# Six buffers for the conditioning rows, loads five tasks ahead, and VectorE's paced operations held in program order

## The chip, the cores and the metric

The kernel runs on one core of one Trainium2 chip. The metric is the device time of one execution in microseconds. In this text the engines are called as the profile calls them: PE is TensorE (PEld its weight loads), DVE is VectorE, ACT is ScalarE, POOL is GpSimd, and SP is SyncE, which here only issues DMAs. L152 is line 152 of the kernel.

## The reference

A two-layer diffusion backbone works on 256 latent tokens of width 2048, with 256 context tokens beside them. Everything is float32. Layer 0 mixes tokens by neighbourhood attention (16 heads), layer 1 by a gated MLP whose spatial weights mix positions in chunks of 128. Each mixer is followed by a SwiGLU FFN of inner width 5632. Every sub-layer is modulated by a condition vector c:

```python
sh1, sc1, g1, sh2, sc2, g2 = split(silu(c) @ ada_w[i] + ada_b[i], 6)
h = layer_norm(ALPHA * h + g1 * mixer(h * (1 + sc1) + sh1), ...)
h = layer_norm(ALPHA * h + g2 * swiglu(h * (1 + sc2) + sh2), ...)
```

The modulation itself is a product of one vector with a matrix of 2048 x 12288 per layer. That matrix is 100 MB per layer, and reading it is a large part of the kernel's 606 MB of traffic from HBM.

## The kernel before, in words

**The main work.** PE multiplies in three passes: each operand is split into a high part (a cast by ACT, L93) and a low part (a subtraction by DVE, L94), and `mm3` (L87 to L90) multiplies high by high, high by low and low by high. Weights stream in as pieces of 128 x 1024 numbers, 512 KB each. SP loads a piece into one of four raw buffers (L110), ACT and DVE split it, and PE uses it in twelve or more matmuls. `piece()` hands out one piece and calls `prefetch`, so that in the code the split of a piece stands four pieces ahead of its use (two during attention, since `pos["bufs"]` is 3 there and 5 later). Activations are split by `act_split` into `gh` and `gl`, with four buffers each.

**The stages.** First come the early products with the first modulation (0 to about 160 us), then attention head by head (to about 600), the output projection, the first FFN (`pg`, `pu`, then `pod`, to about 1411), the gated MLP (`gv`, `gu`, `pogo`, to about 1713) and the second FFN. At the end of each `project_out` the residual, the layer norm and the next modulation run on DVE and ACT, and PE needs their result.

**The paced tasks.** The rest of the modulation is done in small steps beside the main work. There are two kinds of task. A `dot_task` loads 512 KB of the matrix (tile `ad`, L77) and multiplies it with the broadcast condition row, summing over the row (L152). A `gate_task` loads 512 KB (tile `ag`, L77) and adds it, scaled by one column, to a gate tile (L176); after 32 of them a `sum_task` adds up the gate's partitions on POOL (L191). There are 192 tasks of the first kind and 128 of the second. All their loads go through ACT's DMA queue into tiles with the tag `ada`, of which there are four. `junk` (L335) and the tiles `e` in `project_out` share that tag, at other times.

`add_tasks` fills a list at four places in the code: the start of attention, the first FFN, the gated MLP and the second FFN. `tick()` is called after the products of a piece. It adds credit at a rate set by `pace` and runs tasks while there is credit; when `side` holds other work (row-wise affine work, transposes) it runs one item of that and counts 0.3 of a tick. `need(...)` runs all tasks that are left of the named vectors at once. `fetch_ahead` issues the loads of the first `FETCH` tasks of the list.

**What sets the order.** The code is only a list of instructions. When the program is built, a planner gives each engine a fixed order. It goes by priority (the order in the code, or ahead of it inside `tc.high_priority`) and by the times at which it assumes that inputs are there. An instruction that is ready may pass earlier ones that are not. `pin` (`keep_in_program_order`) forbids one thing: a pinned instruction is not placed ahead of the instruction that precedes it in the code on its own engine. Other instructions may still pass a pinned one. In the kernel before, the loads of the tasks are pinned on ACT (L77), most weight loads of the first stage are pinned on SP, and the DVE operations of the tasks are not pinned. [...]

[...]

Of the kernel before, what the change touches and what calls it, by code (L numbers as in the profile page):

```python
# [15 lines left out]
ALU = mybir.AluOpType  # L16
# [21 lines left out]
SH1, SC1, G1, SH2, SC2, G2 = range(6)  # L38
HK0 = 3
RAW = 4  # L40
ADA = 4
FETCH = 3
BUSY = 0.3
DVE0 = 3
W0 = HK0 * P + 512
# [6 lines left out]
def hybrid_kernel(ctx: ExitStack, tc: tile.TileContext, i, out):  # L52
    nc = tc.nc
    V, S, T = nc.vector, nc.scalar, nc.tensor
# [3 lines left out]
    c_col = outer.tile([P, KT, 2], F32, tag="ccol", name="c_col")  # L58
# [16 lines left out]
    def load(src, name):  # L75
        r = outer.tile([P, 1024], F32, tag="ada", name=name, bufs=ADA)
        tc.keep_in_program_order(nc.scalar.dma_start(r, src))  # L77
        return r
# [5 lines left out]
    def pin(ins):  # L84
        return tc.keep_in_program_order(ins)
# [54 lines left out]
    loaded = {}  # L140

    def dot_task(layer, t, nt, half):
        key = (layer, t, nt, half)

        def fetch():
            src = i["ada_t"][dot_index(layer, t, nt)]
            loaded[key] = load(src[:, half * 1024 : (half + 1) * 1024], f"ad{layer}{t}{nt}{half}")

        def run():
            r = loaded.pop(key)  # L150
            o = (cols2 if half else cols)[:, layer, t, :]
            V.scalar_tensor_tensor(  # L152
                r, r, 1.0, c_bc[:, half * 1024 : (half + 1) * 1024], ALU.mult, ALU.mult,
                accum_out=o[:, nt : nt + 1],
            )
            if nt == KT - 1 and half:
                o = cols[:, layer, t, :]
                V.tensor_tensor(o, o, cols2[:, layer, t, :], ALU.add)
                V.tensor_tensor(o, o, badj[:, layer, t, :], ALU.add)
        return [(layer, t), 0.5, run, fetch]  # L160

    def gate_task(layer, t, kt, half):
        key = (layer, t, kt, half)
        sl = slice(half * 1024, (half + 1) * 1024)

        def fetch():
            if kt == 0 and half == 0:
                g = outer.tile([P, D], F32, tag="gate", name=f"gate{layer}{t}")
                gate[(layer, t)] = g
                nc.gpsimd.memset(g, 0.0)  # L170
                nc.gpsimd.dma_start(g[0:1, :], i["ada_b_row"][layer, t : t + 1, :])
            loaded[key] = load(i["ada_g"][gate_index(layer, t, kt)][:, sl], f"ag{layer}{t}{kt}{half}")

        def run():
            g = gate[(layer, t)][:, sl]
            V.scalar_tensor_tensor(g, loaded.pop(key), c_col[:, kt, 0:1], g, ALU.mult, ALU.add)  # L176
        return [(layer, t), 0.5, run, fetch]

    def act_split(src, name, at=None):
# [17 lines left out]
    def fetch_ahead():  # L197
        for t in tasks[:FETCH]:
            if t[3]:
                t[3]()  # L200
                t[3] = None
# [75 lines left out]
    with tc.tile_pool(name="attnX", bufs=1) as px, ExitStack() as late:  # L277
# [21 lines left out]
        with tc.tile_pool(name="st", bufs=1) as st:  # L299
# [33 lines left out]
            def dot_dve(kt, t):  # L333
                r = held.pop((kt, t))
                junk = outer.tile([P, D], BF16, tag="ada", name=f"junk{kt}", bufs=ADA)  # L335
                for n, (o, bc) in enumerate(((junk, cc_bc), (r, c_bc))):
# [358 lines left out]
    def project_out(kts, src, key, name, finish, extra, last=False):  # L695
        st = stats_tile(name)
        hold = LAST if last else HOLD
        for nh in range(2):
# [10 lines left out]
            def fetch(kt, n):  # L709
                xs = []  # L710
                for k in range(n):
                    at = None
                    if k >= START:
                        if k % 2 == 0:
                            e = outer.tile([P, 4, NT], F32R, tag="ada", name=f"e{name}{k}", bufs=ADA)
                        at = e[:, 2 * (k % 2), :], e[:, 2 * (k % 2) + 1, :]
# [223 lines left out]
def dot_index(layer, t, nt):  # L940
    return DOT[(layer, t, nt)]


def gate_index(layer, t, kt):
    return (layer * 2 + (t == G2)) * KT + kt
# [94 lines left out]
```

## Time and profile before

| | |
|---|---|
| time, median of 3 runs | 2462.59 us (2460.63 to 2463.62) |
| the profiled execution: its time, its span | 2464.19 us, 2462.4 us |
| PE busy | 2388.5 us (97%) |
| DVE busy | 1753.7 us (71%) |
| ACT busy | 1120.5 us (46%) |
| mean granted clock of PE | 0.991 |
| read from HBM | 606.46 MB, 247 GB/s over the span |

The span is the time from the first to the last instruction in the profile. The profiler writes down when each instruction started and ended, which semaphore released it and how long its engine stood idle before it. Ends of matmuls are modelled, so two matmuls in a row overlap in the rows. A row of a group ends with the idle time of the engine just before the group's instructions and with what ended it; a row of the timeline has the same in brackets. A row of a stretch of time lists the busy microseconds of each engine in it, the granted clock of PE as a share of full speed, the share of time in which the DMA engines moved data, and the rate. Idle time of an engine costs nothing as long as the engine that sets the time has work.

### The profile page before, as it was taken

To read this page: it belongs to the slowest core of one execution; us is meant where nothing else is said; L and a number is where in the kernel's file an instruction comes from. 1 tells how busy PE (TensorE), PEld (TensorE's weight loads), DVE (VectorE), ACT (ScalarE), POOL (GpSimd) and SP (SyncE) were. 2 spreads that over 40 slices of the span, in tenths; PEclk is the share of its full clock that TensorE was granted. 3 is DMA by queue.
4 is the path that set the end of the run, shared out by engine and by line. 5 is a ranking of instruction groups with operands and counts; after the bars stand their busy time and mean duration, and the time that the engine had idled before them with its cause. 6 is when DMAs were issued, how large, how long until landed. Compare 5 with 4: busy or idle time off the path is not lost. (4 is left out here: it accounts for less than half of the span.)

```text
span 2462.4 us, 31266 instructions
## 1 busy us (share of the span) xinstructions
PE 2388.5 (97%) x11574; PEld 1979.4 (80%) x11574; DVE 1753.7 (71%) x2158; ACT 1120.5 (46%) x1534; POOL 110.3 (4%) x54
## 2 busy tenths in 40 slices
PE   7999999999999999999999999899999999999998
PEld 5788888888788888887888778777888888888886
DVE  4878877777887777666778778778755555566666
ACT  3344434335554444443455554445544444445453
POOL 0000200000010010000000010020100000020000
PEclk9999999999999999999999999999999999999999
DMA  9978787877578888887888767766567676766563
GB/s 358 346 248 266 254 288 260 273 253 246 188 241 284 293 280 299 284 290 275 280 290 283 247 208 263 241 210 196 199 229 229 226 227 225 230 198 190 178 211 131
DMA packets 167682, 610.63 MB, mean 248 GB/s; under 512 B 19076, under 2 KB 21572, under 8 KB 163172
## 3 DMA queue, kind: packets, MB, share of 16 engines
q1 hardware_dynamic: 120888, 440.64, 53.9%
q10 hardware_dynamic: 46512, 167.96, 19.9%
q8 instruction: 90, 1.47, 0.2%
q14 instruction: 64, 0.52, 0.1%
q0 software_dynamic: 128, 0.03, 0.0%
HBM read 606.46 MB, written 2.10 MB: 247 GB/s over the span
## 5 line engine op out<-in xcount | busy, mean ns | idle before, releaser
L93 ACT CAST hwf<-rwf 128x1024 fp32r<-128x1024 f32 x320 | 336.9, 1053 | 491.2 <-PE pu L90 206.0
L94 DVE TENSOR_TENSOR lwf<-rwf,hwf 128x1024 fp32r<-128x1024 f32 x320 | 404.3, 1277 | 173.8 <-ACT hwf L93 172.8
L152 DVE SCALAR_TENSOR_TENSOR ad<-ad,c_bc 128x1024 f32<-128x1024 f32 x192 | 234.0, 1222 | 168.9 <-DMA ad<-in_ada_t 168.3
L88 PE MATMUL pod<-hwd,ghd 128*128 128x512 f32 x684 | 267.3, 391 | 3.5 <-DVE sg L815 3.5
L90 PE MATMUL pod<-hwd,gld 128*128 128x512 f32 x684 | 266.5, 390 | 0.7 <-DVE gld L94 0.7
L89 PE MATMUL pod<-lwd,ghd 128*128 128x512 f32 x684 | 266.8, 390 | 0.0
L176 DVE SCALAR_TENSOR_TENSOR gate<-ag,c_col,gate 128x1024 f32<-128x1024 f32 x128 | 164.4, 1288 | 121.1 <-DMA ag<-in_ada_g 120.8
L94 DVE TENSOR_TENSOR lwd<-rwd,hwd 128x1024 fp32r<-128x1024 f32 x172 | 211.7, 1232 | 51.3 <-ACT hwd L93 51.0
L93 ACT CAST hwd<-rwd 128x1024 fp32r<-128x1024 f32 x172 | 180.3, 1049 | 33.3 <-PE pu L90 11.5
L88 PEld LDWEIGHTS pod<-hwd,ghd 128*128 128x128 f32 x684 | 128.7, 188 | 30.5 <-DVE sg L815 4.0
L90 PEld LDWEIGHTS pod<-hwd,gld 128*128 128x128 f32 x684 | 128.7, 188 | 28.1 <-DVE gld L94 1.2
L89 PEld LDWEIGHTS pod<-lwd,ghd 128*128 128x128 f32 x684 | 128.8, 188 | 26.6
L88 PE MATMUL pg<-hwf,f1h 128*128 128x512 f32 x320 | 126.4, 395 | 0.0
L88 PE MATMUL pg<-hwf,f0h 128*128 128x512 f32 x320 | 126.4, 395 | 0.0
L90 PE MATMUL pg<-hwf,f1l 128*128 128x512 f32 x320 | 124.7, 390 | 0.0
L90 PE MATMUL pg<-hwf,f0l 128*128 128x512 f32 x320 | 124.7, 390 | 0.0
L88 PE MATMUL pu<-hwf,f0h 128*128 128x512 f32 x320 | 124.5, 389 | 0.0
L89 PE MATMUL pu<-lwf,f0h 128*128 128x512 f32 x320 | 124.5, 389 | 0.0
L90 PE MATMUL pu<-hwf,f0l 128*128 128x512 f32 x320 | 124.5, 389 | 0.0
L88 PE MATMUL pu<-hwf,f1h 128*128 128x512 f32 x320 | 124.5, 389 | 0.0
L89 PE MATMUL pu<-lwf,f1h 128*128 128x512 f32 x320 | 124.5, 389 | 0.0
L90 PE MATMUL pu<-hwf,f1l 128*128 128x512 f32 x320 | 124.5, 389 | 0.0
(338 smaller groups left out, 5345.1 us busy)
## 6 DMA issues: line engine op xcount, KB each, us to landing
rwf<-in_w_in_t SPq DMA_DIRECT2D x320, 512.0 KB
ad<-in_ada_t ACTq DMA_DIRECT2D x192, 512.0 KB
rwd<-in_w_out SPq DMA_DIRECT2D x176, 512.0 KB
ag<-in_ada_g ACTq DMA_DIRECT2D x128, 512.0 KB
rwg<-in_w_gin SPq DMA_DIRECT2D x64, 512.0 KB
ap<-in_ada_p SPq DMA_DIRECT2D x19, 1024.0 KB
rwq<-in_w_q SPq DMA_DIRECT2D x32, 512.0 KB
rwo<-in_w_o SPq DMA_DIRECT2D x32, 512.0 KB
```

Of the source, the lines that this page charges most:

```text
L88: keep(T.matmul(ps, sh, mh, start=first, stop=False))
L89: keep(T.matmul(ps, sh, ml, start=False, stop=False))
L90: keep(T.matmul(ps, sl, mh, start=False, stop=last))
L93: S.copy(hi, src)
L94: V.tensor_tensor(lo, src, hi.bitcast(F32), ALU.subtract)
L152: V.scalar_tensor_tensor(r, r, 1.0, c_bc[:, half * 1024 : (half + 1) * 1024], ALU.mult, ALU.mult, accum_out=o[:, nt : nt + 1],)
L176: V.scalar_tensor_tensor(g, loaded.pop(key), c_col[:, kt, 0:1], g, ALU.mult, ALU.add)
```

## The change

The tag `ada` gets six buffers instead of four, which takes 8 KB more of each partition, and `FETCH` is 5 instead of 3. [...] The DVE operations of both kinds of task are wrapped in `pin`.

```diff
-ADA = 4
-FETCH = 3
+ADA = 6
+FETCH = 5
+SCRATCH = 4096
...
-            V.scalar_tensor_tensor(
+            pin(V.scalar_tensor_tensor(
                 r, r, 1.0, c_bc[:, half * 1024 : (half + 1) * 1024], ALU.mult, ALU.mult,
                 accum_out=o[:, nt : nt + 1],
-            )
+            ))
...
-            V.scalar_tensor_tensor(g, loaded.pop(key), c_col[:, kt, 0:1], g, ALU.mult, ALU.add)
+            pin(V.scalar_tensor_tensor(g, loaded.pop(key), c_col[:, kt, 0:1], g, ALU.mult, ALU.add))
...
-    nc = bacc.Bacc("TRN2", target_bir_lowering=False, num_devices=1)
+    nc = bacc.Bacc("TRN2", target_bir_lowering=False, num_devices=1, dynamic_dma_scratch_size=SCRATCH)
```

## The prediction

> **What bounds the kernel now.** I read the shares of the engines first, then the groups of the paced operations, then the stages, then the places where PE stands still. The page:
>
> ```profile
> PE 2388.5 (97%) x11574; PEld 1979.4 (80%) x11574; DVE 1753.7 (71%) x2158; ACT 1120.5 (46%) x1534; POOL 110.3 (4%) x54
> ...
> L152 DVE SCALAR_TENSOR_TENSOR ad<-ad,c_bc 128x1024 f32<-128x1024 f32 x192 | 234.0, 1222 | 168.9 <-DMA ad<-in_ada_t 168.3
> ...
> L176 DVE SCALAR_TENSOR_TENSOR gate<-ag,c_col,gate 128x1024 f32<-128x1024 f32 x128 | 164.4, 1288 | 121.1 <-DMA ag<-in_ada_g 120.8
> ```
>
> PE sets the time. The 320 paced operations of VectorE (DVE) that the change touches make DVE wait 168.3 + 120.8 = 289.1 us for their loads, but a wait of DVE costs only where PE then runs dry. By stage (columns: stretch, length, busy us and instructions of PE, PEld, DVE, ACT, POOL, clock, DMA share, GB/s):
>
> ```profile
> 164.00:700.00 536.00, 514.77 (x2746) 441.41 (x2745) 415.95 (x613) 247.09 (x402) 18.87 (x6) 0.99 0.76 251
> 700.00:1165.00 465.00, 465.00 (x2092) 384.93 (x2090) 331.97 (x352) 197.56 (x212) 20.45 (x7) 1.00 0.85 287
> ```
>
> From 700 to 1165 PE never stops: nothing can be won there, whatever DVE waits. Losses sit in attention and around the changes of stage. Windows of 10 us on them, in the same columns:
>
> ```profile
> 385.00:395.00 10.00, 7.62 (x42) 6.96 (x41) 9.80 (x19) 5.17 (x10) 0.00 (x0) 0.84 0.68 227
> 515.00:525.00 10.00, 7.36 (x37) 6.62 (x36) 9.98 (x18) 5.27 (x10) 0.00 (x0) 0.83 0.51 184
> 560.00:570.00 10.00, 7.65 (x49) 6.76 (x48) 9.61 (x18) 5.17 (x10) 0.00 (x0) 1.00 0.56 178
> 1165.00:1175.00 10.00, 6.46 (x25) 5.10 (x25) 6.75 (x9) 2.56 (x5) 0.00 (x0) 0.83 0.76 222
> 1435.00:1445.00 10.00, 7.35 (x26) 5.57 (x25) 5.79 (x8) 3.67 (x6) 1.45 (x2) 0.83 0.43 148
> 1545.00:1555.00 10.00, 6.72 (x23) 5.38 (x23) 8.47 (x9) 2.16 (x3) 0.50 (x1) 0.83 0.70 198
> 1560.00:1570.00 10.00, 6.97 (x28) 5.28 (x27) 7.08 (x10) 3.27 (x7) 0.00 (x0) 0.83 0.75 261
> 1612.00:1622.00 10.00, 8.07 (x41) 6.39 (x40) 6.47 (x9) 4.26 (x6) 0.00 (x0) 1.00 0.61 205
> 268.00:278.00 10.00, 5.11 (x23) 4.52 (x24) 10.00 (x15) 4.67 (x7) 5.08 (x1) 0.83 0.36 115
> 194.00:204.00 10.00, 8.32 (x51) 7.14 (x50) 9.38 (x14) 5.64 (x12) 0.00 (x0) 1.00 0.90 305
> ```
>
> PE idle in the first eight is 10 minus PE busy: 2.38 + 2.64 + 2.35 + 3.54 + 2.65 + 3.28 + 3.03 + 1.93 = 21.8 us. Six of them also show a clock of 0.83 or 0.84, that is 1.6 or 1.7 us lost to a halved clock behind the stall: 10.1 us. What stood on DVE just before (columns: start, length, operation, idle time and who ended it):
>
> ```profile
> 512.77 1.23 DVE L152 SCALAR_TENSOR_TENSOR ad<-ad,c_bc 128x1024 f32<-128x1024 f32 x1 [4.18 <-DMA ad<-in_ada_t]
> ...
> 515.02 1.23 DVE L152 SCALAR_TENSOR_TENSOR ad<-ad,c_bc 128x1024 f32<-128x1024 f32 x1 [1.01 <-DMA ad<-in_ada_t]
> ...
> 516.17 0.76 DVE L535 TENSOR_TENSOR s<-s,bias 128x256 f32<-128x256 f32 x2
> ```
> ```profile
> 384.08 1.23 DVE L152 SCALAR_TENSOR_TENSOR ad<-ad,c_bc 128x1024 f32<-128x1024 f32 x1 [2.30 <-DMA ad<-in_ada_t]
> ```
> ```profile
> 558.50 1.23 DVE L152 SCALAR_TENSOR_TENSOR ad<-ad,c_bc 128x1024 f32<-128x1024 f32 x1 [4.26 <-DMA ad<-in_ada_t]
> ```
> ```profile
> 1165.60 1.23 DVE L152 SCALAR_TENSOR_TENSOR ad<-ad,c_bc 128x1024 f32<-128x1024 f32 x1 [2.31 <-DMA ad<-in_ada_t]
> ```
> ```profile
> 1436.93 1.28 DVE L176 SCALAR_TENSOR_TENSOR gate<-ag,c_col,gate 128x1024 f32<-128x1024 f32 x1 [4.46 <-DMA ag<-in_ada_g]
> ```
> ```profile
> 1562.12 1.29 DVE L176 SCALAR_TENSOR_TENSOR gate<-ag,c_col,gate 128x1024 f32<-128x1024 f32 x1 [2.83 <-DMA ag<-in_ada_g]
> ```
> ```profile
> 1616.54 1.28 DVE L176 SCALAR_TENSOR_TENSOR gate<-ag,c_col,gate 128x1024 f32<-128x1024 f32 x1 [1.89 <-DMA ag<-in_ada_g]
> ```
>
> Seven of the eight have a paced operation that holds DVE for a load while something that PE needs (scores, `sg`, `m1l`, `u`) queues behind it. The eighth, at 1548, waits for a weight's split:
>
> ```profile
> PE gu L89 <- DVE lwg L94: 3.3, 1, 3.3
> ```
>
> **Why the loads are late.** The code loads three tasks ahead. The trace of the last block shows what became of that:
>
> ```profile
> L77 ACTq DMA_DIRECT2D ag<-in_ada_g x29: 334/334/367, 1760.1 to 2160.2; - x29
> L176 DVE SCALAR_TENSOR_TENSOR gate<-ag,c_col,gate x29: 1276/1285/1286, 1770.0 to 2166.3; 128x1024 f32<-128x1024 f32 x29
> ```
>
> A task comes every (2160.2 - 1760.1) / 28 = 14.3 us, so three tasks ahead would be 43 us. Yet the first operation follows its own load by 9.9 us and the last by 6.1. The load is held at its place in the code, the operation is not: the planner moved it forward until it stood right behind the landing that it assumed. At 512 the same shows: by their order in the code, the two operations belong behind `lwq` of the piece after the scores' one.
>
> **The change part by part.** [...]
>
> *Six buffers, five ahead.* The 320 loads and their bytes stay, one load per finished task, so the rate stays; only at each of the four starts of a task list five loads go out instead of three, 1.05 MB more, 3.6 us at 287 GB/s. Hidden by weight buffers where they are full. Bounds 0 and 4 x 3.6 = 14; I take 1, nearer to nothing because the stage rows leave 15 to 24% of the DMA free. ACT's issue of load n+5 waits for operation n-1, as n+3 did before, so ACT is held no longer.
>
> *The pins.* They add a rule to the planner, no instruction: each paced operation stands behind the DVE instruction that precedes it in the code. Mostly that is the weight split four pieces ahead (two in attention), so the operation comes late enough for its load and still before PE needs the next split. All eight stalls lose their cause except the one at 1548: there the weights queue on SP behind row loads that wait for the affine work on DVE. Four gate operations now wait ahead of that work, here the first and the last of them, and move behind it:
>
> ```profile
> 1503.96 1.29 DVE L176 SCALAR_TENSOR_TENSOR gate<-ag,c_col,gate 128x1024 f32<-128x1024 f32 x1 [1.49 <-DMA ag<-in_ada_g]
> ...
> 1519.75 1.28 DVE L176 SCALAR_TENSOR_TENSOR gate<-ag,c_col,gate 128x1024 f32<-128x1024 f32 x1 [2.21 <-DMA ag<-in_ada_g]
> ```
>
> Bounds 0 and 3.28 + 1.7 = 5.0; I take half. Gain: 21.8 + 10.1 - 2.5 = 29.4. The window at 194 (1.68 idle, a gate operation ahead of a `lwv`) makes it 31.1. The one at 268 is left: its split was held by the reduction, and that stays; 0 to 4.9 + 1.7 = 6.6, taken as 0.
>
> The clock term rests on rows such as 515 to 525: 2.64 us idle, clock 0.83. [...]
>
> What the pins cost. First, the end of the first FFN: `begin` asks for all remaining tasks. Of 129 tasks 127 are paced out by then (250 ticks, less 10 side items x 0.7, at 64.5 / 245 a tick, half a unit each), so two remain. Moved forward, they ran some 22 us ahead of that place (the last at 1381.7); pinned, they stand behind the `std` of the last residual, ahead of the moments on which PE waits:
>
> ```profile
> L152 DVE SCALAR_TENSOR_TENSOR ad<-ad,c_bc x96: 1214/1225/1229, 873.4 to 1381.7; 128x1024 f32<-128x1024 f32 x96
> ```
> ```profile
> 1407.35 0.69 DVE L605 BATCH_NORM_STATS2 std<-h_t 128x6 f32<-128x512 f32 x1
> 1408.07 0.26 DVE L609 BATCH_NORM_AGGREGATE mvm<-std 128x2 f32<-128x24 f32 x1
> ```
> ```profile
> 1410.78 0.41 PE L665 MATMUL ztm<-ident,h_t 128*128 128x128 f32 x2 [2.22 <-DVE h_t L623]
> ```
> ```profile
> L158 DVE TENSOR_TENSOR cols<-cols,cols x6: 166/170/175, 368.3 to 1383.1; 128x16 f32<-128x16 f32 x6
> ```
>
> Two x (1.22 + 0.08 for the accumulator) plus two small additions of 0.17 = 2.9 us, on the path, because PE already idles there. Bounds 0 (PE may be given other products) and 2.9; I take 2.9.
>
> Second, each gate list ends with a reduction on POOL that holds DVE:
>
> ```profile
> 1638.61 12.78 POOL L191 PARTITION_ALL_REDUCE gate<-gate  x1 [93.11 <-DVE gate L176]
> ```
> ```profile
> 1639.61 9.30 DVE L94 TENSOR_TENSOR glgo<-uT,ghgo 128x256 fp32r<-128x256 f32 x1
> ```
>
> A split of 0.42 us took 9.3. The cover is four weight pieces of 2.72 us (the two `lwd` rows below are one piece apart), 10.9. Pinned behind the eleventh `glgo` (this very row), the last gate operation comes 3 to 6 us later and the reduction ends by about 1657, with the residual at 1666: still in time, but DVE catches up later. -1 to +6, I take 2. In the last FFN the list ends behind a `lwd`:
>
> ```profile
> 2205.72 1.23 DVE L94 TENSOR_TENSOR lwd<-rwd,hwd 128x1024 fp32r<-128x1024 f32 x1 [1.49 <-ACT hwd L93]
> 2208.44 1.22 DVE L94 TENSOR_TENSOR lwd<-rwd,hwd 128x1024 fp32r<-128x1024 f32 x1 [1.49 <-ACT hwd L93]
> 2209.59 1.28 DVE L815 TENSOR_TENSOR sg<-pu,sg 128x512 f32<-128x512 f32 x2
> ```
>
> So the reduction moves from steady work to the change of stage at 2208, beside `sg`. 0 to 5, I take 2.
>
> The sum against the profiled execution: 2464.2 - 31.1 + 1 + 2.9 + 2 + 2 = 2441.0. It lies 1.6 above the median of 2462.6, so the forecast is 2439. With all bounds at their good ends the gain is 31.1 + 2.5 + 6.6 + 1 = 41 (2421); at their bad ends 31.1 - 2.5 - 14 - 2.9 - 6 - 5 = 0.7 (2462).
>
> **Rivals.** *Deeper:* the stalls at 268 and 1548 go too and the reductions cost nothing: 2424. For it: both hang on the order that is replanned. Against: nothing that the change does shortens the reduction.
>
> *Loads collide:* the bursts take the weights' share. Casts do wait for weights already:
>
> ```profile
> ACT hwf L93 <- DMA rwf<-in_w_in_t: 71.2, 32, 7.3
> ```
>
> At 14 us for the four starts instead of 1 the time is 2452. Against: buffers stand full there. [...]
>
> *Nothing:* the stalls pass to the next link (scores to exp on ACT, loads for the splits): within 5 us, 2460. It is also what comes of a pin that the planner can satisfy without moving the operation, because its predecessor is early as well. Against: DVE's idle time in the fences above is 2 to 4 us, as long as PE's.
>
> *Slower:* in attention DVE is 416 of 536 us busy, and pinned operations may no longer fill the holes in which DVE waits for PE; they come in pairs right ahead of a head's score chain. If the pair (2 x 1.22) and a halved clock (1.7) are exposed in each of 13 heads, that is 54 us against 31: 2486. It decides from 8 heads on. For it: the pairs are written ahead of the scores. Against: today they run ahead of them too, and pay the load besides; and the pin sets them behind a split, which lets ready scores pass.
>
> **How the numbers follow.** The forecast's case (2428 to 2450) gets 0.60, deeper 0.13, loads collide 0.10, nothing 0.07, slower 0.10. A difference under 0.2% (4.9 us) can't be told from none. So faster 0.83, same 0.07, slower 0.10. The range 2420 to 2460 leaves out about 0.05 below and 0.12 above.
>
> **What would show it.** In the profile after: waits of DVE for `ad` and `ag` under 60 us in all (289 now); the first eight windows, found by their stage, without PE idle over 1 us; the operations of the last FFN 40 us or more behind their loads; two `ad` operations directly ahead of `mvm` and a longer wait of `ztm`; reductions near 1643 and 2207. The prediction is wrong if those waits vanish and PE's idle sum stays, or if new PE waits for `p`, `sg` or weights of more than 15 us in all appear.

## The result and the profile after

The kernel after takes 2449.31 us (median, 2447.53 to 2451.58) against 2462.50 us of the kernel before beside it. The ratio is 0.9949, 95% interval 0.9932 to 0.9965: faster by 13 us, where 24 were forecast; the time lies at the upper edge of the forecast's own case (2428 to 2450). The profiled execution's span went from 2462.4 to 2449.8 us.

The page of the kernel after, its engines and the groups of the two paced operations (all line numbers stand one higher than before):

```profile
PE 2384.6 (97%) x11574; PEld 1977.0 (81%) x11574; DVE 1765.5 (72%) x2158; ACT 1123.0 (46%) x1534; POOL 106.3 (4%) x54
...
L153 DVE SCALAR_TENSOR_TENSOR ad<-ad,c_bc 128x1024 f32<-128x1024 f32 x192 | 230.7, 1218 | 5.2 <-DMA ad<-in_ada_t 5.2
L177 DVE SCALAR_TENSOR_TENSOR gate<-ag,c_col,gate 128x1024 f32<-128x1024 f32 x128 | 163.1, 1281 | 3.4 <-DMA ag<-in_ada_g 3.3
```

DVE's waits for the loads fell from 289.1 to 8.5 us. In the last FFN the operations now stand far behind their loads, 34.9 us at the first and 73.9 us at the last (4.0 and 6.1 before, over the same 32). First the kernel after, then the kernel before:

```profile
L78 ACTq DMA_DIRECT2D ag<-in_ada_g x32: 334/335/450, 1706.3 to 2110.2; - x32
L177 DVE SCALAR_TENSOR_TENSOR gate<-ag,c_col,gate x32: 1276/1280/1282, 1741.2 to 2184.1; 128x1024 f32<-128x1024 f32 x32
```
```profile
L77 ACTq DMA_DIRECT2D ag<-in_ada_g x32: 334/334/450, 1728.2 to 2160.2; - x32
L176 DVE SCALAR_TENSOR_TENSOR gate<-ag,c_col,gate x32: 1276/1285/1286, 1732.2 to 2166.3; 128x1024 f32<-128x1024 f32 x32
```

So 281 us of DVE's waiting went and 13 us of time came back. The stages tell where. A stretch here runs from the start of a stage's first matmul to that of the next stage's; "forecast" puts the prediction's terms into the stretch in which they lie.

| stretch, us | before | after | gain | forecast |
|---|---|---|---|---|
| start to attention (`qps`) | 160.8 | 161.4 | -0.6 | 0 |
| attention to `powo` | 413.6 | 401.9 | 11.7 | 12.3 |
| `powo` to first FFN's `pg` | 94.1 | 93.9 | 0.2 | 0 |
| `pg` to `pod` | 493.7 | 495.4 | -1.7 | 0 |
| `pod` to `gv` | 251.6 | 248.5 | 3.2 | 5.2 - 2.9 = 2.3 |
| `gv` to `gu` | 98.1 | 96.2 | 1.9 | 4.4 |
| `gu` to `pogo` | 103.5 | 98.5 | 5.0 | 7.2 |
| `pogo` to second FFN's `pg` | 98.6 | 97.6 | 1.1 | 1.9 - 2 = -0.1 |
| `pg` to `pod` | 495.7 | 493.7 | 2.0 | 0 |
| `pod` to the end | 252.5 | 262.7 | -10.2 | -2 |
| load bursts, anywhere | | | | -1 |
| sum | 2462.4 | 2449.8 | 12.6 | 23.1 |

Over the whole span PE's idle time fell by 8.7 us (73.9 to 65.2) and its busy time, for the same 11574 matmuls, by 3.9 us (2388.5 to 2384.6).

Windows of the kernel after, set by stage (later places come up to 20 us earlier now), in the columns of the prediction's (stretch, length, busy us and instructions of PE, PEld, DVE, ACT, POOL, clock, DMA share, GB/s):

```profile
268.00:278.00 10.00, 4.26 (x14) 3.08 (x13) 9.85 (x9) 1.72 (x3) 8.13 (x1) 0.76 0.36 118
382.00:392.00 10.00, 10.00 (x62) 8.89 (x62) 8.39 (x15) 5.88 (x12) 0.00 (x0) 1.00 0.86 301
508.00:518.00 10.00, 10.00 (x66) 9.07 (x65) 8.44 (x15) 6.44 (x11) 0.00 (x0) 1.00 0.83 295
550.00:560.00 10.00, 8.65 (x58) 7.74 (x57) 8.55 (x16) 5.66 (x9) 0.00 (x0) 1.00 0.59 214
1150.00:1160.00 10.00, 8.95 (x41) 6.78 (x40) 8.47 (x11) 5.00 (x6) 0.00 (x0) 1.00 0.88 299
1390.00:1400.00 10.00, 6.03 (x30) 4.62 (x29) 9.87 (x22) 6.83 (x11) 2.25 (x2) 0.98 0.42 156
1400.00:1410.00 10.00, 8.81 (x31) 6.69 (x32) 7.06 (x17) 6.51 (x16) 0.60 (x1) 0.68 0.52 154
1430.00:1440.00 10.00, 7.33 (x33) 5.75 (x32) 8.92 (x11) 3.18 (x4) 2.73 (x3) 1.00 0.32 97
1540.00:1550.00 10.00, 7.08 (x28) 5.47 (x27) 8.76 (x12) 5.43 (x8) 0.00 (x0) 0.83 0.93 346
1592.00:1602.00 10.00, 10.00 (x49) 7.97 (x47) 7.51 (x11) 5.53 (x8) 0.00 (x0) 1.00 0.78 271
2190.00:2200.00 10.00, 3.69 (x11) 3.03 (x12) 8.41 (x5) 1.13 (x2) 7.54 (x2) 0.58 0.28 79
```

The windows at 382, 508 and 1592, where PE stood still before, are full. Those at 550 and 1150 keep 1.4 and 1.1 us idle of 2.4 and 3.5, and all five have full clock. The window at 268 is a little poorer than before, two of the gated MLP (1430, 1540) still have holes, those from 1390 to 1410 show the end of the first FFN, and the last row is a hole that was not there before. What PE waits for, in the kernel after (total, times, longest):

```profile
PE pod L89 <- DVE sg L816: 8.8, 3, 7.7
...
PE kps L91 <- DVE lwk L95: 6.0, 2, 5.7
...
PE ztm L666 <- DVE h_t L624: 3.0, 1, 3.0
PE sp L882 <- DVE u L883: 2.9, 1, 2.9
PE gv L90 <- DVE lwg L95: 2.7, 1, 2.7
...
PE vps L90 <- DVE lwv L95: 1.5, 1, 1.5
PE o L89 <- DVE tl L95: 1.4, 1, 1.4
```

The new hole, as POOL, DVE and PE have it (timeline of the kernel after):

```profile
2185.46 11.88 POOL L192 PARTITION_ALL_REDUCE gate<-gate  x1 [441.15 <-DVE gate L177]
```
```profile
2184.08 1.28 DVE L177 SCALAR_TENSOR_TENSOR gate<-ag,c_col,gate 128x1024 f32<-128x1024 f32 x1
2185.66 10.00 DVE L95 TENSOR_TENSOR lwd<-rwd,hwd 128x1024 fp32r<-128x1024 f32 x1 [0.30 <-ACT hwd L94]
2195.58 1.27 DVE L816 TENSOR_TENSOR sg<-pu,sg 128x512 f32<-128x512 f32 x2
```
```profile
2196.31 0.80 PE L89 MATMUL pod<-hwd,ghd 128*128 128x512 f32 x1 [7.70 <-DVE sg L816]
```

The last gate operation ends, the reduction starts, the next split takes 10.00 us instead of 1.2, and `sg`, on which PE waits with no piece in reserve, stands behind that split. In the kernel before, the same reduction had stood 42 us ahead of the change of stage (at 2209.9); now it stands 1.6 us ahead of it (at 2187.1):

```profile
2167.72 12.77 POOL L191 PARTITION_ALL_REDUCE gate<-gate  x1 [400.73 <-DVE gate L176]
```

### The profile page after: what moved, and what is told of

The parts are those of the page before. It is cut to its first block, busy times and chain, and to the rows that moved or that the text cites. A ratio compares the mean times of both kernels' runs of the same rounds, so it can differ in the third digit from the quotient of the medians.

```text
span 2449.8 us, 31278 instructions
## 1 busy us (share of the span) xinstructions
PE 2384.6 (97%) x11574; PEld 1977.0 (81%) x11574; DVE 1765.5 (72%) x2158; ACT 1123.0 (46%) x1534; POOL 106.3 (4%) x54
## 4 chain that ended last, share of the span: by engine, by line
PE 90%; DVE 5%; DMA 2%; ACT 1%; issue 1%; SPq 0%; ACTq 0%; DVEq 0%; POOL 0%; POOLq 0%
PE pg L89 6%; PE pg L91 6%; PE pg L90 6%; PE pod L89 6%; PE pod L91 6%; PE pod L90 6%; PE pu L90 6%; PE pu L91 6%; PE pu L89 6%; PE vps L89 2%; PE vps L90 2%; PE vps L91 2%; PE kps L90 2%; PE kps L91 2%; PE kps L89 2%
## 5 line engine op out<-in xcount | busy, mean ns | idle before, releaser
L95 DVE TENSOR_TENSOR lwd<-rwd,hwd 128x1024 fp32r<-128x1024 f32 x172 | 220.5, 1283 | 67.8 <-ACT hwd L94 67.6
L94 ACT CAST hwd<-rwd 128x1024 fp32r<-128x1024 f32 x172 | 180.1, 1047 | 27.3 <-DMA rwd<-in_w_out 10.8
L90 PEld LDWEIGHTS pod<-lwd,ghd 128*128 128x128 f32 x684 | 129.0, 189 | 26.4
```

The source lines that it names most:

```text
L90: keep(T.matmul(ps, sh, ml, start=False, stop=False))
L94: S.copy(hi, src)
L95: V.tensor_tensor(lo, src, hi.bitcast(F32), ALU.subtract)
```

## The experiments

Theory: the pins alone bring the gain, since they let the operations fall behind their loads; the two extra buffers do nothing; and about 10 us are given back where the second FFN's reduction meets `sg`. Rivals: the depth is what lets the operations wait without harm; or the 10 us belong to VectorE's load there and not to the reduction. Each ratio is against runs of the kernel before on the same chip. The stretches of the profiled executions, in us:

| stretch | pins only | buffers only | `ad` pinned | `ag` pinned | after | no reductions |
|---|---|---|---|---|---|---|
| attention | 402.9 | 427.8 | 401.9 | 416.2 | 401.9 | 394.9 |
| first FFN's `pod` to `gv` | 247.2 | 245.6 | 247.8 | 247.9 | 248.5 | 246.7 |
| `gv` to `pogo` | 192.2 | 202.3 | 201.3 | 192.3 | 194.8 | 196.2 |
| `pogo` to `pg` | 98.0 | 96.1 | 99.6 | 97.7 | 97.6 | 95.4 |
| second FFN's `pod` to the end | 262.7 | 251.9 | 252.3 | 262.3 | 262.7 | 252.2 |
| span | 2446.8 | 2471.5 | 2447.7 | 2458.2 | 2449.8 | 2429.3 |

**Pins only.** Both operations pinned; buffers, depth and scratch as before.

```diff
-            V.scalar_tensor_tensor(
+            pin(V.scalar_tensor_tensor(
...
-            V.scalar_tensor_tensor(g, loaded.pop(key), ...)
+            pin(V.scalar_tensor_tensor(g, loaded.pop(key), ...))
```

> The pins alone, with four buffers, three tasks ahead and the old scratch. Theory (the pins bring the gain, since without them an operation follows its own load whatever the depth): three tasks at two per 5.44 us are 8 us of lead, little over the 6 to 7 us that a load took before, so the waits of DVE for ad and ag fall from 289 to 20 to 60 us and the time is 2449 to 2454 us. Rival (the depth brings the gain): waits over 150 us and 2458 to 2463 us.

Measured: 2447.40 us, ratio 0.9924 (0.9900 to 0.9949). Its rows of the paced operations:

```profile
L152 DVE SCALAR_TENSOR_TENSOR ad<-ad,c_bc 128x1024 f32<-128x1024 f32 x192 | 230.7, 1217 | 3.1 <-DMA ad<-in_ada_t 3.0
...
L176 DVE SCALAR_TENSOR_TENSOR gate<-ag,c_col,gate 128x1024 f32<-128x1024 f32 x128 | 163.5, 1284 | 2.7 <-DMA ag<-in_ada_g 2.7
```

With four buffers the waits are as small as with six. The pins bring all of the gain, a little more than the theory had (20 us of waits at the least, 2449 us).

**Buffers only.** The change without the two `pin`s.

```diff
-ADA = 4
-FETCH = 3
+ADA = 6
+FETCH = 5
+SCRATCH = 4096
```

> Six buffers, five tasks ahead and the small scratch, without the pins. Theory: the planner moves each operation forward behind its load again; the waits of DVE for ad and ag stay at 220 to 300 us and the time at 2458 to 2466 us. Rival (the depth brings the gain): waits under 100 us and 2448 to 2454 us.

Measured: 2475.50 us, ratio 1.0040 (1.0022 to 1.0058), a little slower, and above the 2466 that the theory allowed. Rows of its groups, and of its last FFN:

```profile
L153 DVE SCALAR_TENSOR_TENSOR ad<-ad,c_bc 128x1024 f32<-128x1024 f32 x192 | 233.8, 1221 | 171.3 <-DMA ad<-in_ada_t 170.7
...
L177 DVE SCALAR_TENSOR_TENSOR gate<-ag,c_col,gate 128x1024 f32<-128x1024 f32 x128 | 164.0, 1287 | 99.4 <-DMA ag<-in_ada_g 99.0
```
```profile
L78 ACTq DMA_DIRECT2D ag<-in_ada_g x32: 334/334/450, 1738.4 to 2142.7; - x32
```
```profile
L177 DVE SCALAR_TENSOR_TENSOR gate<-ag,c_col,gate x32: 1272/1284/1287, 1742.0 to 2148.5; 128x1024 f32<-128x1024 f32 x32
```

The loads are issued two tasks earlier in the code, and the free operations move forward with them: 3.6 us behind the load at the first, 5.8 us at the last. DVE waits nearly as before (269.7 us). Attention, 14 us longer than before, is where it loses: PE stands idle there for 26.4 us (17.9 before) and half clock lasts 27.3 us (10.2 before). Which of its orders does that was not taken apart.

**One kind pinned at a time**, with four buffers: first the `ad` operations, then the gate operations.

```diff
 # `ad` pinned
-            V.scalar_tensor_tensor(
+            pin(V.scalar_tensor_tensor(
                 r, r, 1.0, c_bc[:, half * 1024 : (half + 1) * 1024], ALU.mult, ALU.mult,
...
 # gate operations pinned
-            V.scalar_tensor_tensor(g, loaded.pop(key), ...)
+            pin(V.scalar_tensor_tensor(g, loaded.pop(key), ...))
```

> The kernel before with the pin on the column products (the `ad` operations, line 152) alone; the gate operations (line 176) stay free. Theory that each kind of operation waits only for its own loads' place in the program: VectorE's wait for `ad`, 168.3 us before, goes below 30 us, that for `ag` stays above 60 us. In attention the stalls of 2.5 us at 390, 521 and 567 us stand among `ad` operations (the gate operations end near 260 us), so attention comes down by most of its 11 us and the gated MLP, whose paced operations are gate operations, keeps its 103 us: some 2449 to 2453 us. Rival: the unpinned gate operations are now hoisted past the pinned ones and the gain of the first goes to the second; then the time is within 5 us of the kernel before.

Measured: 2450.14 us, ratio 0.9936 (0.9914 to 0.9958). `ad` waits 3.3 us, `ag` 104.1; attention has its whole gain (401.9), the gated MLP keeps its time (201.3 against 201.6), and the second FFN's end has no hole (252.3).

> The kernel before with the pin on the gate operations (line 176) alone. Theory: the wait for `ag`, 120.8 us before, goes below 30 us and that for `ad` stays above 100 us; attention keeps its stalls at 390, 521 and 567 us, the gated MLP and its projection fall by 5 to 8 us: some 2453 to 2458 us. Rival: pinning either kind sets the order for both, and this one too stands near 2447 us.

Measured: 2464.07 us, ratio 0.9993 (0.9977 to 1.0009); the profiled span is 2458.2. `ag` waits 2.8 us, `ad` 163.5. The gated MLP falls by 9 us, as much as with all pins, and the second FFN's end rises by 10: the wait for `sg` is back.

```profile
PE pod L88 <- DVE sg L815: 10.0, 2, 7.7
```

The expectation missed the time because it left that stall out. The two kinds act in different stretches: `ad` pays in attention, `ag` in the gated MLP. From the first FFN's `pod` to `gv` every variant is 3 to 6 us shorter than before (251.6), buffers only included, so that gain is not shown to be the pins'. And the pin on the gate operations also moves the last reduction to the change of stage (2153.3 with them free, 2194.2 with them pinned), which takes back all that they gain.

**The reduction moved.** The kernel after, with the second FFN's pace at 150 units, so that its gate list ends earlier.

```diff
-    pace(170)
+    pace(150)
```

> The changed kernel with the task list of the second FFN paced over 150 units instead of 170, so that its last operation and the reduction on POOL come some 50 us before the change of stage from pu to pod. Theory (the reduction holds a split on DVE and with it sg, and PE stands still for sg): the stall of 7.7 us and its halved clock vanish, 2437 to 2441 us. Rival (the stall of sg has another cause, or a reduction costs PE as much wherever it falls): 2446 to 2451 us.

Measured: 2440.20 us, ratio 0.9899 (0.9872 to 0.9926). From `pod` to the end it takes 252.1 us. The reduction now runs at 2132.43 and holds a split about as long, one of the four in the second row here (DVE, timeline), but before a stretch of steady work:

```profile
2131.05 1.28 DVE L177 SCALAR_TENSOR_TENSOR gate<-ag,c_col,gate 128x1024 f32<-128x1024 f32 x1
2132.63 13.40 DVE L95 TENSOR_TENSOR lwf<-rwf,hwf 128x1024 fp32r<-128x1024 f32 x4 [0.30 <-ACT hwf L94]
2145.96 0.68 DVE L816 TENSOR_TENSOR sg<-pu,sg 128x512 f32<-128x512 f32 x1
```

PE waits for `sg` nowhere. The same hold costs 10 us or nothing, by its place.

**No reductions.** The kernel after without the four sums over partitions; the gates stay unsummed, and all else is done.

```diff
-            g = gate[(layer, t)]
-            nc.gpsimd.partition_all_reduce(g, g, P, ReduceOp.add)
+            pass
```

> The changed kernel without the four reductions of the gate rows over the partitions: the gates are left unsummed, so the output is not the reference's, and all else is done. Theory: a reduction on GpSimd holds the VectorE operation issued beside it some 9 us, and PE pays where the next wait on VectorE has no slack. It gives back the 7.9 us stall near 2196 with its low clock (10.4 us in all) and the 5.9 us stall near 274 with its low clock (7 to 9 us), and little for the other two: 2430 to 2434 us. Rival that these stalls belong to VectorE's load of work there and not to the reduction: the change-of-stage stall near 2196 stays above 4 us and the span above 2442 us.

Measured: 2430.10 us, ratio 0.9864 (0.9834 to 0.9894); the kernel after on the same chip 2447.99, so the four together cost 18 us. The second FFN's end is at 252.2, attention at 394.9 (7 less), the gated MLP's projection some 2 less. The rival falls: with the same work on DVE and no reduction, PE is full in both places.

```profile
262.00:272.00 10.00, 10.00 (x70) 9.13 (x69) 9.69 (x19) 6.55 (x12) 0.00 (x0) 1.00 0.99 363
2178.00:2188.00 10.00, 10.00 (x49) 8.29 (x48) 8.56 (x8) 6.55 (x12) 5.40 (x2) 1.00 0.48 158
```

**The left-over tasks.** The kernel after, with the first FFN's pace at 232, so that no task is left when `begin` asks for all.

```diff
-    pace(245)
+    pace(232)
```

> The changed kernel with the task list of the first FFN paced over 232 units instead of 245, so that no task is left when the end of that FFN asks for them. Theory (the two left-over operations lie ahead of the moments on the path of PE): the chain at the end of the first FFN is 2.4 to 3 us shorter, 2445 to 2448 us. Rival (PE is given other products meanwhile, or operations paced closer cost elsewhere): 2449 to 2452 us.

Measured: 2443.91 us, ratio 0.9912 (0.9885 to 0.9938). In the kernel after, DVE shows the two tasks just where they were forecast, ahead of the moments (`mvm`):

```profile
1391.63 1.21 DVE L153 SCALAR_TENSOR_TENSOR ad<-ad,c_bc 128x1024 f32<-128x1024 f32 x1
...
1392.76 1.22 DVE L153 SCALAR_TENSOR_TENSOR ad<-ad,c_bc 128x1024 f32<-128x1024 f32 x1
...
1393.91 0.26 DVE L610 BATCH_NORM_AGGREGATE mvm<-std 128x2 f32<-128x24 f32 x1
```

With the pace at 232 the wait for `h_t` is gone and the stretch to `gv` is 243.4 us, 5.0 less. The next one is 91.7, another 4.5 less: the half clock behind the stall (0.68 in the window 1400 to 1410) and the `lwg` stall at 1434 are gone too. That the latter belongs to the tasks is not shown, since it is also absent with pins only, where the two tasks still run. The output projection gives 3.4 back. The gain is more than the 2.4 to 3 us expected, and not all of it is the price of the tasks. Against the kernel before, they made PE's wait for `h_t` longer by 0.8 us (2.2 to 3.0) and the half clock behind it by 3.4 us (3.4 to 6.8); with the pace at 232 the 2.2 us that the kernel before had there without any task ahead went as well (0.2 left).

**All of it together**, on one chip: the kernel after once more, then both paces with six buffers, and with four.

```diff
-    pace(245)
+    pace(232)
...
-    pace(170)
+    pace(150)
```

> The changed kernel itself once more, beside the other three. The pins with six buffers should again stand at 0.993 to 0.997 of the kernel before; with that as the mark, the rest of these runs is read. Its span should again hold the stall of 7.9 us near 2196 and the one of 3.1 us near 1398.

> The changed kernel with both paces moved: 245 to 232 in the first FFN and 170 to 150 in the second. Theory: the two stalls lie in different stages and each move mends its own, so the gains add: the span of 2449.8 us less 10.6 (second FFN's pace alone) less 8.2 (first FFN's pace alone) is 2431 us, a ratio near 0.988 to 0.984. Rival: what the earlier pace freed (the first reductions and gate operations done sooner) is the same slack that the later pace uses; then the span stays at 2437 to 2440 us.

> The kernel before with the two pins and both paces, and with its four buffers, loads three tasks ahead and its own scratch. Theory that the depth is worth nothing once the operations are pinned: within 4 us of the kernel with six buffers and both paces, 2428 to 2435 us. Rival that the depth only pays once the stalls are gone and the operations come closer together: VectorE's waits for ad and ag come back above 30 us and the span is 6 us or more above that kernel's.

Measured, against 2465.46 us before:

| kernel | us | ratio (95%) | span |
|---|---|---|---|
| after, again | 2447.99 | 0.9934 (0.9913 to 0.9955) | 2445.8 |
| after, both paces | 2433.22 | 0.9874 (0.9850 to 0.9898) | 2432.5 |
| pins, four buffers, both paces | 2433.36 | 0.9873 (0.9849 to 0.9898) | 2431.5 |

The two gains add: 2449.8 less 10.6 and 8.2 us is 2431.0, and the span is 2432.5. Depth is worth nothing here either. Two pins and two changed numbers on the kernel before give all of it.

**Two more paces**, each on top of the pins with four buffers and both FFN paces: attention's, to bring the first reduction out of its stall, and the gated MLP's, to thin out its gate operations.

```diff
 # attention
-        pace(126)
+        pace(118)
...
 # gated MLP
-    pace(62)
+    pace(70)
```

> The kernel before with both pins, the two moved paces of the first and second FFN, and attention's pace moved from 126 to 118, so that the first reduction comes some 6 us earlier. Theory that the 6 us stall near 274 us is the reduction meeting a head's chain of weight splits by chance: moved into a stretch where PE has weights ahead, it costs under 3 us and attention falls by 4 us or more, to below 399 us. Rival that every place in a head's 25 us meets such a chain: the stall moves with the reduction and attention stays within 2 us of 402.

Measured: 2433.01 us, ratio 0.9870 (0.9849 to 0.9891); attention 402.2 us against 402.6. The reduction moved to 259.22 and the stall with it, from a wait for `lwk` to one for `p`. The rival is right:

```profile
PE pt L552 <- ACT p L542: 7.8, 1, 7.8
```

> The same kernel (both pins, both moved FFN paces), with attention's pace at 126 and the gated MLP's moved from 62 to 70, so that its 32 gate operations stand further apart. Theory that the stalls of 3.3 us near 1536 us (PE waits for `u`) and of 2.5 us near 1645 us come from VectorE being full of gate operations and weight splits, not from loads: with fewer operations per piece the stretch from the gate's own matmuls to the output projection falls from 98.1 us by 3 to 6 us. Rival: the third reduction now comes later, into the output projection's tail, and gives back the same or more, so that the sum of the two stretches (98.1 and 99.3 us) stays or rises.

Measured: 2444.51 us, ratio 0.9912 (0.9893 to 0.9932). `gu` to `pogo` stays at 98.6 us and the projection rises from 99.3 to 109.5, with the third reduction at 1629.30 instead of 1617.92. PE waits longer there, and half clock lasts 17.1 us of that stretch where there was none:

```profile
PE pogo L90 <- DVE glgo L94: 5.3, 2, 3.7
```

The theory falls, and its rival is right. The wait of `sp` for `u` is 3.3 us with fewer gate operations too, so neither loads nor the number of gate operations make it. What does stays open.

## Why the prediction was right, and where it was not

**The cause was right.** The operations were free, stood right behind their loads' assumed landing, and moved forward with any deeper load: with the pins alone 5.7 us of waits are left, with the depth alone 269.7. The prediction gave the buffers no gain, and they have none. The size was not right: 13 us of 24, and the terms below show where it went.

**Attention's sum came out**: 12.3 us forecast, 11.7 measured. The half clocks behind 390 and 521, priced at 3.3 us, are gone, while the one behind the stall at 268 grew from 3.4 to 6.8 us; PE's idle time fell by 8.5 us (17.9 to 9.4), where 9.05 had been added up (2.38 + 2.64 + 2.35 + 1.68). It is not right item by item, so part of the agreement is luck: the wait for `lwv` near 198, counted as won, stayed (1.5 us), one of 1.4 us for `tl` came in the last head, and small waits that weren't counted went (for `lwq` at 172 and `lwk` at 289, each about 1 us).

**The mis-sized term is "the reduction moves from steady work to the change of stage at 2208, beside `sg`: 0 to 5, I take 2".** The place was right, the price is 10 us: 10.2 us by the stretch, 10.6 by moving it away, 10.6 by leaving it out. The cover that the prediction had counted for a reduction, four weight pieces or 10.9 us, doesn't help here: `sg` is not a weight that was split ahead, PE needs it at once, and it queues behind the held split. A stall of 7.7 us then takes 10.24 us of half clock with it (2191.56 to 2201.80), of which 5.5 us lie behind the stall: 7.7 + 2.7 = 10.4. The bound should have been the hold that the prediction's own row showed, 9.3 us, plus a clock term.

**The gated MLP gained less**: 6.9 us from `gv` to `pogo` against 11.6 forecast (8.0 in the second profile of the kernel after, 9.5 with pins only, where `gv` to `gu` has its whole 4.4). The wait at `gu`'s first weights is gone but for 0.2 us, where half was hoped for. But the one for `m1l` near 1435 passed to the next link, `lwg` (2.7 us), and the one for `u` near 1560 stayed (2.9 us): there the load was only one of the things in line. Of the eight stalls six are gone or down to about 1 us, not seven.

**The left-over tasks** were foretold to the instruction, and their stretch gained 3.2 us where 2.3 were forecast. The price of 2.9 us is not contradicted: beside the kernel before they cost 0.8 us of wait and 3.4 us more of half clock, that is 1.7 us. The 5 us that their removal brings include a wait that the kernel before had without them.

**The stall at 268** stayed, as taken. It belongs to the first reduction, and neither the pins nor the one other pace that was tried end it.

**The rivals.** Deeper fell: the reductions' cost grew. Loads collide fell: with the pins the depth makes no difference (2433.2 and 2433.4 us). Buffers alone do lengthen the first FFN's `pg` to `pod` by 4.3 us, but where PE stands there (1.9 us at 875.3) it waits for an `sg` behind a split that the second reduction held, not for a load. Slower fell for the pins: attention gained 11.7 us, with the pairs where they were feared. The link that took over, `sg`, was foreseen: the sign of failure was over 15 us of new waits for `p`, `sg` and weights together. In the kernel after `sg` has 8.8 us, `lwk` 6.0, `lwg` 2.9 and `lwv` 1.5, of which only `sg`'s 7.7 stand where PE had not waited before.

**The other signs.** DVE's waits (8.5 us, under 60 asked for), the two `ad` operations and the places of the two reductions came as named. Not met were the 40 us of distance in the last FFN (34.9 at the first operation) and the limit of 1 us in the eight windows, which four of them exceed.

**Readings that were off, without effect.** The 9.9 us between load and operation belong to the fourth gate task of the last FFN; the first stood 4.0 us behind. What the `SCRATCH` of the diff costs by itself no run shows; both paces moved, the time is 2433.2 us with it and six buffers, and 2433.4 without it and with four. By its own terms the rival "deeper" gives 2426 (2439 - 6.6 - 2.5 - 4), not 2424.

## What to carry to other kernels

Where a DMA is issued at its place in the code and the operation on it is free to move, look at the time between issue and operation: if it is short and doesn't grow with depth (here 4.0 us at the first operation of the last FFN with loads three tasks ahead, 3.6 with five), order is missing, not buffers. When work is re-timed, follow the last item of its list too: here a reduction at the end of the list moved by 40 us of the main work, from 42 to 1.6 us ahead of a change of stage, and took back as much as one of the two pins had gained. The price of a hold on another engine was about its whole length where PE needed the very next result (10 us), and nothing in a stretch with pieces in reserve (no wait for `sg` behind the splits at 2132.63).

## What the runs showed of the hardware

**Half clock began on a fixed grid.** All 102 stretches of half clock in the 14 traces begin, within each trace, on a grid of 3.413 us that doesn't follow the stalls: before, 391.76, 521.47 and 1170.00 lie 38 and 190 steps apart, (521.47 - 391.76) / 38 = 3.413. Over the 14 traces (100 to 2400 us) I added up PE's idle time in each window of that grid that itself had full clock, for those with over 0.9 us. With under 1.59 us, none of 104 was followed by half clock (before none of 8, after none of 8); from 1.59 to 1.95, 11 of 28 (2 of 4, 1 of 3); above, 57 of 57 (7 of 7, 4 of 4). So in these traces a window over 57% idle was followed by half clock every time and one from 47% on sometimes, and a stall counted or not by how the grid cut it. Two pairs of neighbouring windows in the kernel after, then three in the kernel before:

```profile
1430.39:1433.80 3.41, 1.50 (x7) 0.92 (x5) 2.72 (x3) 1.86 (x3) 1.79 (x2) 1.00 0.00 1
1433.80:1437.22 3.42, 2.66 (x12) 2.20 (x13) 3.42 (x5) 0.00 (x0) 0.00 (x0) 1.00 0.44 135
1543.03:1546.44 3.41, 0.75 (x4) 0.65 (x5) 3.01 (x5) 1.78 (x3) 0.00 (x0) 1.00 1.01 381
1546.44:1549.86 3.42, 3.42 (x13) 2.69 (x11) 2.76 (x5) 1.30 (x3) 0.00 (x0) 0.50 0.78 261
```
```profile
562.43:565.84 3.41, 1.87 (x10) 1.43 (x8) 3.41 (x8) 1.45 (x4) 0.00 (x0) 1.00 0.37 111
565.84:569.26 3.42, 2.61 (x22) 2.59 (x23) 3.42 (x7) 3.39 (x6) 0.00 (x0) 1.00 0.48 146
518.06:521.47 3.41, 0.78 (x7) 0.53 (x6) 3.41 (x7) 1.91 (x6) 0.00 (x0) 1.00 0.51 164
521.47:524.88 3.41, 3.41 (x18) 3.41 (x18) 3.41 (x7) 2.86 (x5) 0.00 (x0) 0.50 0.18 66
1412.35:1415.76 3.41, 1.70 (x6) 0.97 (x6) 3.38 (x9) 3.41 (x8) 2.08 (x1) 1.00 0.48 154
1415.76:1419.17 3.41, 3.41 (x9) 2.63 (x8) 3.41 (x8) 3.41 (x6) 0.50 (x1) 0.50 0.35 117
```

The stalls at 1434 and 565 are split by the grid (1.91 and 1.54 us idle in the first window) and cost no clock; those at 1545 and 521 fall into one window (2.66 and 2.63) and the next is at 0.50. In the last pair 1.71 us were enough.

**POOL's reduction held only some of DVE.** Beside reductions of 11.88 us in the kernel after, splits, which read two tiles that are both in SBUF, took 10.00 (at 2185.66, 1.21 to 1.23 for its neighbours) and 7.39 us (at 266.52, 0.67 to 0.69 for the three others of its size). `oT`, which reads a product from PSUM, ran in 0.68 us at 265.93, 1.7 us after the reduction at 264.25 had begun and just ahead of the split that it held. That the memory they read is what decides was not tested by itself. The hold also ended before the record did: at 273.91 a split ran in 1.20 us, while that reduction stands on record until 276.13 (264.25 + 11.88).
